# Band masks of a windowed attention: from identity products on TensorE to additions on VectorE

## The chip, the cores and the metric

The kernel runs on one core of one Trainium2 chip. The metric is the device time of one execution in microseconds; lower is better. A core has TensorE (PE, with its weight loads as PEld), VectorE (DVE), ScalarE (ACT), GpSimd (POOL) and SyncE (SP, which issues most DMAs). Every engine works through its own list of instructions in the order in which the build put them there, and waits on semaphores for the others.

## The reference

Two layers over 1024 latent tokens and 256 context tokens, model width 1024, all in float32. Layer 0 (even) has two attentions side by side, A (global) and B (windowed), each with 8 query heads on 2 key heads of width 64. What matters here is B: blocks of 128 queries look at the 256 context keys and at a band of three key blocks, of which keys farther than 128 positions are masked, and a learned sink logit joins the softmax.

```python
def gqa_attend(q, k, v, bias=None, sink=None):
    s = jnp.einsum("bqhgd,bkhd->bhgqk", q, k) * ATTN_SCALE      # ATTN_SCALE = 1/8
    if bias is not None:
        s = s + bias
    ...                                                          # sink column, softmax
    return jnp.einsum("bhgqk,bkhd->bqhgd", p, v)

# B: one block of 128 queries, band of 3 key blocks
rel = jnp.arange(band)[None, :] - B_WINDOW - jnp.arange(Q_BLOCK)[:, None]
in_band = jnp.abs(rel) <= B_WINDOW
bias = jnp.concatenate([ctx_open, jnp.where(valid, 0.0, NEG_INF)], axis=-1)
```

Of the three key blocks the middle one lies wholly in the window; the block before it and the block behind it are each masked along a triangle. Layer 1 (odd) has a convolution branch and a neighbourhood attention D whose scores get a full bias table.

## The kernel before

**Matmuls in split precision.** A float32 operand is split into a high part in the format of the products (fp32r in the profile) and a low part (`split`, lines 325 to 334: a cast on ACT, a subtraction on POOL or DVE). Three products replace one.

**Attention, `attn_gen`.** One generator runs all attention of a layer as a list of groups; a group is four heads of one key head against one block of 128 queries (layer 0), so a score tile is 128 keys by 512 (4 heads x 128 queries). For each tile, in this order: two matmuls into a PSUM bank `st` (L529 keys by `QH`; L533 keys and four extra rows by `QL`, which brings the low part of the query and minus the row's maximum), the exponential on ACT from the bank into the SBUF tile `pf` (L541, scale 1/8), the split of `pf` into `ph` (ACT, L331) and `pl` (POOL or DVE, L334), and, three tiles later (`LOOK0`), the products with the values into bank `ov` (L480 to L482). There are two `st` banks, two `pf` buffers (tag `ost` in layer 0) and four each of `ph` and `pl`.

**Masks before.** A masked tile of layer 0 gets a third matmul into its bank between L529 and L533 (L532): the mask tile `bmt` (two 128x128 triangles, 0 or a large negative number) as weights, the identity, repeated for four heads, as the moving operand. In layer 1 the neighbourhood bias already goes another way: DVE adds it from the bank to `pf` (L538), and ACT takes the exponential in place (L539).

**What stands beside it.** The key heads are worked in the order `ORDER = (2, 3, 0, 1)`: units 2 and 3 are B, 0 and 1 are A. `weave` alternates steps of the attention with steps of a filler: the projection of the next unit (`pq`, `pg` matmuls L352 to L354; transposes `trk` L932, casts and rotary work on DVE: L906 to L922, L334 on `qs` and `KAt`). Per group, `attn_prep` and `attn_fin` find row maxima ahead of the scores: matmuls into a bank `mx` (L643, L663), DVE reductions (L645, and L664 with the mask), a chain of small DVE operations on `nmt` and `se` (L439 to L446), a transpose on PE (`trn`, L457), and DVE's write of the result into `QL` (L458), which L533 needs. The end of a group is DVE's too (L490 to L493, L693, L695).

**What sets the order.** A list scheduler in the build orders each engine's instructions by priority and by its own estimates of cost. So an edit moves neighbours as well. 14 of the tiles of each B unit are masked, 28 in all.

Of the kernel before, what the change touches and what calls it, by code (L numbers as in the profile page):

```python
# [10 lines left out]
F32 = mybir.dt.float32  # L11
F32R = mybir.dt.float32r
ALU = mybir.AluOpType
AF = mybir.ActivationFunctionType
# [4 lines left out]
P = 128  # L19
# [5 lines left out]
SCALE = 0.125  # L25
# [53 lines left out]
QORD = (2, 3, 4, 0, 5, 6, 1, 7, 8, 9)  # L79
# [10 lines left out]
def tile_kernel(ctx: ExitStack, tc: tile.TileContext, a, out):  # L90
    nc = tc.nc
    VE, SC, GP, PE, SY = nc.vector, nc.scalar, nc.gpsimd, nc.tensor, nc.sync
# [20 lines left out]
    def nm(s):  # L113
        uid[0] += 1
        return f"{s}_{uid[0]}"
# [11 lines left out]
    identr = cp.tile([P, P], F32R, tag="ident", name="ident")  # L127
# [193 lines left out]
    acts, dmas, firstq = [], [], []  # L321

    @contextmanager
    def behind():

        with tc.issue_after(acts[-1].ins):
            yield
# [84 lines left out]
    def copy_k(k):  # L412
        KA, KB = Ks[k % len(Ks)]
        with behind():
            acts.append(SC.copy(KB[0:64, :], KA[0:64, :].bitcast(F32)))
# [47 lines left out]
    def attn_gen(pool, groups, vshare, look, nexts=None):  # L463

        preps = [g.prep for g in groups]
        items = [(g, t) for g in groups for t in range(len(g.tiles))]
        pend = []
        cnt = [0]

        def flush():  # L470
            g, t, ph, pl = pend.pop(0)
            k, q0, n, _ = g.tiles[t]
            if t == 0:
                g.ov = bank("ov", nm("ov"))
                if g.load_v is not None:
                    g.load_v()
            V = g.v(k)
            last = t == len(g.tiles) - 1
            o = g.ov[:, q0 : q0 + n]
            PE.matmul(o, V[:, 64:192], ph[:, :n], start=(t == 0), stop=False)  # L480
            PE.matmul(g.ov[0:64, q0 : q0 + n], V[:, 0:64], ph[:, :n], start=False, stop=False)  # L481
            PE.matmul(o, V[:, 64:192], pl[:, :n], start=False, stop=(last and g.sink is None))  # L482
            if last:
                if g.sink is not None:
                    PE.matmul(g.ov, g.skm(), g.QL[0:76, :], start=False, stop=True)
                r1 = pool.tile([P, 8, 32], F32, tag="r1", name=nm("r1"), bufs=1)
                r8 = pool.tile([P, 8], F32, tag="r8", name=nm("r8"), bufs=2)
                rb = pool.tile([P, 256], F32, tag="rb", name=nm("rb"), bufs=1)
                for e in range(2):
                    VE.transpose(r1[e * 64 : (e + 1) * 64].rearrange("p a b -> p (a b)")  # L490
                                 .rearrange("p (a q) -> p a q", a=2), g.den(g.ov[64:128, :], e))
                VE.reciprocal(r8, r1[:, :, 0])
                VE.transpose(rb, r8[:, :, None].broadcast_to([P, 8, 32]))  # L493
                g.finish(g.ov, rb)

        if layer[0]:
            for g in groups[:3]:
                queries(g, kvs[-1])
        for p in preps[:2]:
            for n_, _ in enumerate(p):  # L500
                if n_ % 2:
                    yield
        for _ in attn_fin(groups[0]):
            pass
        if layer[0]:
            groups[0].copy()
        for gi, g in enumerate(groups):
            ids = [gi + 2] if gi + 2 < len(groups) else []
            if nexts is not None and gi in nexts:
                ids = nexts[gi]  # L510
            nx = [preps[k] for k in ids]
            if gi + 1 < len(groups):
                nx.insert(1 if ids[:1] == [gi + 1] else 0, attn_fin(groups[gi + 1]))
            g.next = chain.from_iterable(nx)
            g.step = -(-(18 * len(ids) + 4) // len(g.tiles))
        for g, t in items[:AHEAD]:
            g.ahead(t)
        for x, (g, t) in enumerate(items):
            if x + AHEAD < len(items):
                items[x + AHEAD][0].ahead(items[x + AHEAD][1])  # L520
            if t == 0:
                g.start()
                if layer[0] and g.no + 3 < len(groups):
                    queries(groups[g.no + 3], kvs[-1])
            k, q0, n, extra = g.tiles[t]
            KA, KB = g.k()
            st = bank("st", nm("st"))
            cs = slice(k * P, (k + 1) * P)
            sts.append(PE.matmul(st[:, :n], KA[:, cs], g.QH[:, q0 : q0 + n], start=True, stop=False))  # L529
            if not g.bias:  # L530
                for lhs, rhs in extra():
                    PE.matmul(st[:, :n], lhs, rhs, start=False, stop=False)  # L532
            PE.matmul(st[:, :n], KB[0:68, cs], g.QL[0:68, q0 : q0 + n], start=False, stop=True)  # L533
            ph = pool.tile([P, 512], F32R, tag="ph", name=nm("ph"), bufs=look + 1)
            pl = pool.tile([P, 512], F32R, tag="pl", name=nm("pl"), bufs=look + 1)
            pf = pool.tile([P, 512], F32, tag="pf" if layer[0] else "ost", name=nm("pf"), bufs=PFB)
            if g.bias and extra is not None:
                VE.tensor_tensor(pf[:, :n], st[:, :n], extra(), op=ALU.add)  # L538
                acts.append(SC.activation(pf[:, :n], pf[:, :n], AF.Exp))  # L539
            else:  # L540
                acts.append(SC.activation(pf[:, :n], st[:, :n], AF.Exp, scale=1.0 if g.bias else SCALE))  # L541
            cnt[0] += 1
            split(pf[:, :n], ph[:, :n], pl[:, :n], "s", "v" if cnt[0] % vshare == 0 else "g")
            pend.append((g, t, ph, pl))
            if t == len(g.tiles) // 2:
                g.gate()
            for _ in range(g.step // 2):
                next(g.next, None)
            yield
            if len(pend) > look:  # L550
                flush()
            for _ in range(g.step - g.step // 2):
                next(g.next, None)
            if t == len(g.tiles) - 1:
                for _ in g.next:
                    pass
            yield
        while pend:
            flush()
            yield  # L560
# [26 lines left out]
    h = [None] * 3  # L587
# [3 lines left out]
    a0 = a0x.enter_context(tc.tile_pool(name="a0", bufs=1, reuse_waits="tile"))  # L591
    sink = const("sink", [P, 8], SC, kvp)
# [3 lines left out]
    KAs, KBs, V0s = [None] * 4, [None] * 4, [None] * 4  # L596
# [13 lines left out]
    def load_kb(u):  # L610

        for ks in (slice(0, 512), slice(512, NTOK)):
            SY.dma_start(KBs[u][0:64, ks].bitcast(F32), KAs[u][0:64, ks].bitcast(F32))
# [7 lines left out]
    def group0(u, qb):  # L621
        isb = u >= 2
# [44 lines left out]
                    yield  # L667

        def mask(m):
            return lambda: [(identr, bmt[:, m, None, :].broadcast_to([P, 4, P]))]  # L670

        def none():
            return []

        kt = [(0, none), (1, none)]
        if qb >= 2:
            if isb:
# [11 lines left out]
        def finish(ov, rb):  # L689
# [9 lines left out]
            else:  # L699
# [2 lines left out]
                split(y, oh[c][0][:, fs, o : o + P], oh[c][1][:, fs, o : o + P], "s", "v")  # L702

        hs = (u - 2) * 4
        g = Group(load_q=load_q, start=(lambda: load_kb(u)) if qb == QORD[0] else (lambda: None), bias=False, ahead=lambda t: None, gate=gate, v=lambda k: V0s[u][:, k, :], load_v=None, maxes=maxes, nmp=1 if qb < 2 else (2 if isb else 3),
                  sink=(sink[:, hs : hs + 4], sink8[:, hs : hs + 4]) if isb else None, skm=lambda: sk, k=lambda: (KAs[u], KBs[u]),
                  tiles=[(k, 0, 512, x) for k, x in kt], den=den, finish=finish)
        g.prep = attn_prep(kvp, g)
# [7 lines left out]
    with ExitStack() as p0x:  # L716
# [94 lines left out]
        with after_mod(4):  # L811
# [3 lines left out]
            VE.tensor_copy(gain5[:, 0:4, :], gain[:, None, 0:64].broadcast_to([P, 4, 64]))  # L815
            VE.tensor_copy(gain5[:, 4, :], gain[:, 64:128])
            bmask = const("k_bm", [P, 384], SY, a0)
        bmt = a0.tile([P, 2, P], F32R, tag="bmt", name="bmt")
        sk = a0.tile([76, P], F32R, tag="sk", name="sk")
        cst = a0.tile([P, 512], F32, tag="ost", name="cst", bufs=2)  # L820
        with after_mod(4):
# [147 lines left out]
        for k in range(4):  # L969
            u = ORDER[k]  # L970
            n = NSTEP[u // 2] + (12 if k == 0 else 0)
# [140 lines left out]
    with ExitStack() as l1x:  # L1112
# [242 lines left out]
        def group1(gi, hd, hf):  # L1355
            i, e = divmod(hd, 2)
            ds = slice(e * 64, (e + 1) * 64)
            bms, bss = {}, {}
# [58 lines left out]

            tiles = [(0, 0, 512, None)]
            for t, (r0, r1) in enumerate(QROWS):
                tiles.append((2 + 5 * hf + t, r0 * 32, (r1 - r0) * 32, lambda t=t: bss[t]))  # L1420
            tiles.append((1, 0, 512, None))

            def den(dn, k):
# [2 lines left out]
            def finish(ov, rb):  # L1426
# [6 lines left out]
                if i == 3:  # L1433
                    split(y[ds], od3[hf][ds, 0], od3[hf][ds, 1], "s", "v")

            g = Group(no=gi, copy=lambda: copy_k(hd), load_q=load_q, load_b=load_b, maxes=maxes, nmp=2, bias=True, ahead=ahead, sink=None, tiles=tiles, den=den, finish=finish,
                      start=start, gate=gate,
                      k=lambda: Ks[hd % len(Ks)], load_v=None, v=lambda k: Vs[gi % 2][:, k if k < 2 else k - 5 * hf, :])
            g.prep = attn_prep(kvs[-1], g)
# [295 lines left out]
```

## Time and profile before

| | |
|---|---|
| runs (3) | 1527.92, 1532.71, 1538.26 us; median 1532.71 |
| profiled execution | span 1528.5 us from its first to its last instruction; the page gives no other time for it |
| median of the runs above that span | 4.2 us |
| mean granted TensorE clock | 0.976 |
| PE busy | 1451.0 us, 95% of the span |
| PEld / DVE / ACT / POOL busy | 1167.2 / 1031.7 / 748.1 / 788.0 us |
| masked tiles' mask matmuls (L532) | 28, first at 153.6 us, last at 486.6 us |

The span and what lies around it make up a run's time; since the three runs themselves lie 10.3 us apart, the 4.2 us are no more than their scatter. A matmul's bar in the trace is longer than the time for which it holds up the next one, because matmuls overlap: the spacing of starts is the price, not the bar. In tables of stretches each engine has its busy time and, in brackets, the number of instructions; PEclk is the share of full clock that TensorE was granted.

### The profile page before, as it was taken

What the parts mean: (1) busy time and instruction counts of PE and PEld (TensorE: products, weight loads), DVE (VectorE), ACT (ScalarE), POOL (GpSimd) and SP (SyncE); (2) the same over time, 40 slices, a digit from 0 to 9 for tenths busy, and PEclk for the clock granted to TensorE, in tenths of its full rate; (3) what the DMA queues carried; (4) which work ended last, traced back from release to release, by engine and by line L of the source; (5) the groups of instructions that cost most, each with busy time, mean ns of one, the idle gap of its engine ahead of it and who ended that gap; (6) DMA issues with size and microseconds to landing.
All of it is one profiled execution on the core that took longest, in us unless ns stands there. A gap on an engine that the chain in (4) does not pass through costs nothing.

```text
span 1528.5 us, 21545 instructions
## 1 busy us (share of the span) xinstructions
PE 1451.0 (95%) x7144; PEld 1167.2 (76%) x7144; DVE 1031.7 (67%) x2095; ACT 748.1 (49%) x1418; POOL 788.0 (52%) x628
## 2 busy tenths in 40 slices
PE   6999999998998999999999889999999999989996
PEld 2786877896896777886777568888887788868775
DVE  2643566589578856457676948899848666567766
ACT  3642433443435564447646665343334455455564
POOL 3360443555454766557645665665532434364665
PEclk9999999999999999999999999999999999989998
DMA  9564325422312246121202021210484677877642
GB/s 366 201 225 135 106 69 174 135 77 88 114 56 76 85 138 210 49 69 54 59 28 66 35 67 56 62 56 28 158 253 144 207 219 240 248 222 234 178 129 110
DMA packets 154167, 199.83 MB, mean 131 GB/s; under 512 B 14716, under 2 KB 95816, under 8 KB 154056
## 3 DMA queue, kind: packets, MB, share of 16 engines
q1 hardware_dynamic: 147392, 186.88, 38.9%
q10 hardware_dynamic: 6664, 11.57, 2.3%
q8 instruction: 56, 0.92, 0.3%
q14 instruction: 55, 0.45, 0.1%
HBM read 148.07 MB, written 49.02 MB: 129 GB/s over the span
## 4 chain that ended last, share of the span: by engine, by line
PE 79%; DVE 11%; issue 3%; DMA 3%; ACT 2%; POOL 1%; ACTq 0%; SPq 0%; DVEq 0%; POOLq 0%
PE p L352 6%; PE p L354 6%; PE p L353 6%; PE ov L480 5%; PE ov L482 4%; PE ov L481 4%; PE po L352 4%; PE st L533 4%; PE st L529 4%; PE po L353 4%; PE po L354 4%; PE pq L352 4%; PE pq L353 3%; PE pq L354 3%; PE pg L352 2%
## 5 line engine op out<-in xcount | busy, mean ns | idle before, releaser
L334 POOL TENSOR_TENSOR pl<-pf,ph 128x512 fp32r<-128x512 f32 (+4 forms) x321 | 394.0, 1239 | 384.9 <-ACT ph L331 337.3
L541 ACT ACTIVATE pf<-st 128x512 f32<-128x512 f32 x284 | 166.5, 597 | 203.6 <-PE st L533 165.2
L334 POOL TENSOR_TENSOR wl<-wr,wh 128x512 fp32r<-128x512 f32 (+2 forms) x131 | 169.3, 1302 | 136.5 <-ACT wh L331 124.0
L331 ACT CAST ph<-pf 128x512 fp32r<-128x512 f32 (+4 forms) x364 | 209.5, 588 | 27.1 <-PE ov L481 15.9
L352 PE MATMUL p<-hh,wh 128*128 128x512 f32 x448 | 176.0, 393 | 3.4 <-DVE spq L1233 1.3
L353 PE MATMUL p<-hl,wh 128*128 128x512 f32 x448 | 174.5, 390 | 0.0
L354 PE MATMUL p<-hh,wl 128*128 128x512 f32 x448 | 173.0, 391 | 0.0
L480 PE MATMUL ov<-ph,Vt 128*128 128x512 f32 (+4 forms) x364 | 141.0, 387 | 4.2 <-DVE y L693 2.0
L529 PE MATMUL st<-QH,KAt 128*128 128x512 f32 (+4 forms) x364 | 140.2, 386 | 3.9 <-ACT pf L541 3.1
L482 PE MATMUL ov<-pl,Vt 128*128 128x512 f32 (+4 forms) x364 | 141.1, 388 | 2.2 <-POOL pl L334 2.1
L481 PE MATMUL ov<-ph,Vt 128*64 128x512 f32 (+4 forms) x364 | 138.9, 381 | 0.0
L533 PE MATMUL st<-QL,KBt 68*128 68x512 f32 (+4 forms) x364 | 136.4, 386 | 0.9 <-issue 0.8
L1177 DVE SCALAR_TENSOR_TENSOR cps<-U,taps,cps 128x512 f32<-128x512 f32 x184 | 125.9, 748 | 0.7
L331 ACT CAST wh<-wr 128x512 fp32r<-128x512 f32 (+2 forms) x134 | 80.9, 613 | 84.1 <-PE po L353 15.9
L352 PEld LDWEIGHTS p<-hh,wh 128*128 128x128 f32 x448 | 84.2, 188 | 21.5 <-ACT spq L1231 1.6
L656 DVE TENSOR_REDUCE mp<-mx 128x1 f32<-128x512 f32 x128 | 85.3, 681 | 19.3 <-PE mx L655 18.3
L354 PEld LDWEIGHTS p<-hh,wl 128*128 128x128 f32 x448 | 84.1, 188 | 17.4
L353 PEld LDWEIGHTS p<-hl,wh 128*128 128x128 f32 x448 | 84.2, 188 | 17.1 <-issue 0.2
L1020 DVE SCALAR_TENSOR_TENSOR x<-po,modT,x 128x512 f32<-128x512 f32 (+1 forms) x72 | 46.9, 657 | 64.0 <-PE po L354 63.5
L352 PE MATMUL pq<-wh,hh 128*128 128x384 f32 x256 | 88.2, 344 | 1.0 <-ACT hh L331 1.0
L353 PE MATMUL pq<-wl,hh 128*128 128x384 f32 x256 | 87.3, 341 | 0.0
L354 PE MATMUL pq<-wh,hl 128*128 128x384 f32 x256 | 86.6, 342 | 0.0
(287 smaller groups left out, 3417.2 us busy)
## 6 DMA issues: line engine op xcount, KB each, us to landing
mw<-in_mod_w_dram SPq DMA_DIRECT2D x16, 1024.0 KB, 5.3
Q<-qs SPq DMA_DIRECT2D x40, 256.0 KB, 2.1
QH<-Q SPq DMA_DIRECT2D x80, 128.0 KB, 2.7
mw<-in_mod_w_dram SPq DMA_DIRECT2D x16, 512.0 KB, 6.8
wr<-in_od_d_dram SPq DMA_DIRECT2D x32, 256.0 KB, 3.1
wr<-in_ev_qkv_dram SPq DMA_DIRECT2D x16, 384.0 KB, 5.0
KAt<-KD SPq DMA_DIRECT2D x16, 384.0 KB, 6.5
wr<-in_od_wo_dram SPq DMA_DIRECT2D x22, 256.0 KB, 3.4
```

Source lines behind the costliest of these rows:

```text
L331: acts.append(SC.copy(hi, src))
L334: (GP if leng == "g" else VE).tensor_tensor(lo, src, hi.bitcast(F32), op=ALU.subtract)
L352: PE.matmul(o, lh, rh, start=first, stop=False)
L353: PE.matmul(o, lh, rl, start=False, stop=False)
L354: last.append(PE.matmul(o, ll, rh, start=False, stop=end))
L480: PE.matmul(o, V[:, 64:192], ph[:, :n], start=(t == 0), stop=False)
L481: PE.matmul(g.ov[0:64, q0 : q0 + n], V[:, 0:64], ph[:, :n], start=False, stop=False)
L482: PE.matmul(o, V[:, 64:192], pl[:, :n], start=False, stop=(last and g.sink is None))
L529: sts.append(PE.matmul(st[:, :n], KA[:, cs], g.QH[:, q0 : q0 + n], start=True, stop=False))
L533: PE.matmul(st[:, :n], KB[0:68, cs], g.QL[0:68, q0 : q0 + n], start=False, stop=True)
L541: acts.append(SC.activation(pf[:, :n], st[:, :n], AF.Exp, scale=1.0 if g.bias else SCALE))
L1177: VE.scalar_tensor_tensor(pc, uc, w, pc, op0=ALU.mult, op1=ALU.add)
```

## The change

The mask of a layer-0 tile is no longer multiplied in by TensorE. `extra()` now returns the mask as a view, and one DVE `tensor_tensor` adds it on the way from the bank `st` to `pf`; ACT takes the exponential of `pf` in place, with the scale 1/8 as before. Layer 1 takes the same line, with its bias seen as one head (`nh=1`). Unmasked tiles are as they were: ACT reads the bank. `bmt` is kept in plain float32.

```diff
             sts.append(PE.matmul(st[:, :n], KA[:, cs], g.QH[:, q0 : q0 + n], start=True, stop=False))
-            if not g.bias:
-                for lhs, rhs in extra():
-                    PE.matmul(st[:, :n], lhs, rhs, start=False, stop=False)
             PE.matmul(st[:, :n], KB[0:68, cs], g.QL[0:68, q0 : q0 + n], start=False, stop=True)
...
-            if g.bias and extra is not None:
-                VE.tensor_tensor(pf[:, :n], st[:, :n], extra(), op=ALU.add)
-                acts.append(SC.activation(pf[:, :n], pf[:, :n], AF.Exp))
+            if extra is not None:
+                VE.tensor_tensor(pf[:, :n].rearrange("p (h q) -> p h q", h=g.nh), st[:, :n].rearrange("p (h q) -> p h q", h=g.nh),
+                                 extra(), op=ALU.add)
+                acts.append(SC.activation(pf[:, :n], pf[:, :n], AF.Exp, scale=1.0 if g.bias else SCALE))
             else:
                 acts.append(SC.activation(pf[:, :n], st[:, :n], AF.Exp, scale=1.0 if g.bias else SCALE))
...
         def mask(m):
-            return lambda: [(identr, bmt[:, m, None, :].broadcast_to([P, 4, P]))]
-
-        def none():
-            return []
-
+            return lambda: bmt[:, m, None, :].broadcast_to([P, 4, P])
+
+        none = None
...
-        bmt = a0.tile([P, 2, P], F32R, tag="bmt", name="bmt")
+        bmt = a0.tile([P, 2, P], F32, tag="bmt", name="bmt")
...
-                tiles.append((2 + 5 * hf + t, r0 * 32, (r1 - r0) * 32, lambda t=t: bss[t]))
+                tiles.append((2 + 5 * hf + t, r0 * 32, (r1 - r0) * 32, lambda t=t: bss[t][:, None, :]))
```

Two places show what stands where. The lines of the changed kernel are numbered four lower behind the edit (L530 there is L533 before; L535 is the new addition, L641, L643, L662 are L643, L645, L664 before).

TensorE's list at the first masked tile, `st_1474`, in the first B unit, before:

```order
L353 MATMUL pq_1340<-wl_1176,hc_171 128x384
L529 MATMUL st_1474<-QH_1180,KAt_486 128x512
L532 MATMUL st_1474<-bmt,ident 128x512
L533 MATMUL st_1474<-QL_1181,KBt_484 128x512
L457 MATMUL trn_1370<-ident,nmt_1347 12x128
L643 MATMUL mx_1397<-KAt_486,QH_1382 128x256 x2
L480 MATMUL ov_1493<-ph_1364,Vt_487 128x512
```

and now:

```order
L353 MATMUL pq_1340<-wl_1176,hc_171 128x384
L529 MATMUL st_1474<-QH_1180,KAt_486 128x512
L530 MATMUL st_1474<-QL_1181,KBt_484 128x512
L354 MATMUL pq_1340<-wh_1175,hc_171 128x384
L457 MATMUL trn_1370<-ident,nmt_1347 12x128
L641 MATMUL mx_1397<-KAt_486,QH_1382 128x256 x2
L480 MATMUL ov_1493<-ph_1364,Vt_487 128x512
```

The mask product is gone, and a projection matmul has moved up into its place.

VectorE's list where the projection of the second B unit (`qs`, `KAt`, `rt`, `pc`) meets a group's maxima (`mx`, `m`, `nmt`, `se`), before:

```order
L664 ISA mx_2996,mp_2936<-mx_2996,k_bm 128x384
L664 ISA mp_2936 128x1
L920 TENSOR_TENSOR rt_891_3996<-pc_3842,k_cs 128x320 x2
L664 ISA mx_2999,mp_2936<-mx_2999,k_bm 128x384
L664 ISA mp_2936 128x1
L922 TENSOR_TENSOR pc_3842<-pc_3842,k_cs 128x2x320
L664 ISA mx_3055,mp_2936<-mx_3055,k_bm 128x384
L664 ISA mp_2936 128x1
L334 TENSOR_TENSOR qs_4131<-trk_4127,qs_4131 128x256
L439 TENSOR_REDUCE m_667_3059<-mp_2936 128x4
L441 TENSOR_TENSOR nmt_3058<-m_667_3059,sink_161 128x4
```

and now:

```order
L535 TENSOR_TENSOR pf_3239<-st_3234,bmt 128x512
L662 ISA mx_2999,mp_2936<-mx_2999,k_bm 128x384
L662 ISA mp_2936 128x1
L916 TENSOR_TENSOR rt_891_3996<-pc_3842,k_cs 128x320 x2
L662 ISA mx_3055,mp_2936<-mx_3055,k_bm 128x384
L662 ISA mp_2936 128x1
L334 TENSOR_TENSOR qs_4131<-trk_4127,qs_4131 128x256
L918 TENSOR_TENSOR pc_3842<-pc_3842,k_cs 128x2x320
L439 TENSOR_REDUCE m_667_3059<-mp_2936 128x4
L334 TENSOR_TENSOR KAt_486<-trk_4127,KAt_486 64x128
L535 TENSOR_TENSOR pf_3332<-st_3327,bmt 128x512
L441 TENSOR_TENSOR nmt_3058<-m_667_3059,sink_161 128x4
```

Two additions now stand in this run, one of them between the maximum `m` and the chain on `nmt`, and the rotary work on `rt` and `pc` has moved back by a reduction or two.

More of the change, by code (lines that the diff above doesn't have):

```diff
@@ L704, in group0 @@
         hs = (u - 2) * 4
-        g = Group(load_q=load_q, start=(lambda: load_kb(u)) if qb == QORD[0] else (lambda: None), bias=False, ahead=lambda t: None, gate=gate, v=lambda k: V0s[u][:, k, :], load_v=None, maxes=maxes, nmp=1 if qb < 2 else (2 if isb else 3),
+        g = Group(load_q=load_q, start=(lambda: load_kb(u)) if qb == QORD[0] else (lambda: None), bias=False, nh=4, ahead=lambda t: None, gate=gate, v=lambda k: V0s[u][:, k, :], load_v=None, maxes=maxes, nmp=1 if qb < 2 else (2 if isb else 3),
                   sink=(sink[:, hs : hs + 4], sink8[:, hs : hs + 4]) if isb else None, skm=lambda: sk, k=lambda: (KAs[u], KBs[u]),
@@ L1434, in finish @@
                     split(y[ds], od3[hf][ds, 0], od3[hf][ds, 1], "s", "v")
-            g = Group(no=gi, copy=lambda: copy_k(hd), load_q=load_q, load_b=load_b, maxes=maxes, nmp=2, bias=True, ahead=ahead, sink=None, tiles=tiles, den=den, finish=finish,
+            g = Group(no=gi, copy=lambda: copy_k(hd), load_q=load_q, load_b=load_b, maxes=maxes, nmp=2, bias=True, nh=1, ahead=ahead, sink=None, tiles=tiles, den=den, finish=finish,
                       start=start, gate=gate,
```

## The prediction

> **What bounds the kernel now.** I began with the page: who is busy, and what the chain that ended last is made of.
>
> ```profile
> PE 1451.0 (95%) x7144; PEld 1167.2 (76%) x7144; DVE 1031.7 (67%) x2095; ACT 748.1 (49%) x1418; POOL 788.0 (52%) x628
> PE 79%; DVE 11%; issue 3%; DMA 3%; ACT 2%; POOL 1%; ACTq 0%; SPq 0%; DVEq 0%; POOLq 0%
> ```
>
> TensorE is the bound on the whole, and VectorE is next: 11% of the chain runs over it. The averages don't say what is so where the change sits. So next the line of the mask products, which gives the place, and the forms of the operations there, and the table of stretches for that place and for its worst spots.
>
> ```profile
> L532 PE MATMUL st<-bmt,ident x28: 389/395/403, 153.6 to 486.6; 128*128 128x512 f32 x28
> ```
>
> ```profile
> core 0: us, PE busy (x) PEld busy (x) DVE busy (x) ACT busy (x) POOL busy (x), PEclk, DMA share, GB/s
> 150.00:490.00 340.00, 330.40 (x1702) 277.99 (x1700) 232.48 (x546) 143.42 (x304) 164.37 (x123) 0.98 0.31 99
> 240.00:245.00 5.00, 3.91 (x19) 2.99 (x18) 4.92 (x15) 3.39 (x9) 2.52 (x2) 1.00 0.67 256
> 350.00:355.00 5.00, 2.82 (x14) 1.52 (x13) 4.57 (x11) 1.70 (x6) 2.76 (x2) 1.00 0.40 132
> 370.00:375.00 5.00, 3.38 (x14) 1.79 (x12) 4.77 (x12) 2.08 (x7) 3.94 (x3) 0.88 0.32 107
> 375.00:380.00 5.00, 4.71 (x13) 3.76 (x13) 4.36 (x12) 2.61 (x5) 1.70 (x2) 0.50 0.33 108
> 380.00:385.00 5.00, 5.00 (x22) 4.03 (x21) 2.83 (x7) 0.81 (x3) 0.82 (x1) 0.93 0.25 83
> 460.00:475.00 15.00, 12.46 (x57) 9.71 (x56) 13.23 (x30) 5.87 (x11) 7.12 (x5) 0.93 0.12 35
> 485.00:490.00 5.00, 4.19 (x18) 2.57 (x17) 4.81 (x11) 4.06 (x9) 2.73 (x3) 1.00 0.39 106
> ```
>
> The B units take 340 us. TensorE is idle for 9.6 of them (340 - 330.4), VectorE is 68% busy. So most of the stage is bound by TensorE, and a matmul less is a matmul's time less. But the idle time is not spread: it lies where VectorE has no gap. In the five rows from 240 to 245, 350 to 355, 370 to 375, 460 to 475 and 485 to 490 VectorE is busy 4.92, 4.57, 4.77, 13.23 (of 15) and 4.81 us, and TensorE waits for it. The clock row from 375 to 380 says that such a hole is paid twice: there the granted clock is 0.50.
>
> The timeline of TensorE and of VectorE at the third of these shows how the waiting goes:
>
> ```profile
> 370.45 0.41 DVE L334 TENSOR_TENSOR qs<-trk,qs 128x256 fp32r<-128x256 f32 x1
> 371.26 1.47 DVE L443 SCALAR_TENSOR_TENSOR se<-nmt,sink 128x4 f32<-128x4 f32 x1
> 372.75 0.28 DVE L334 TENSOR_TENSOR KAt<-trk,KAt 64x128 fp32r<-64x128 f32 x1
> 373.19 0.52 PE L932 MATMUL trk<-ident,pc 128*128 128x128 f32 x3 [1.43 <-DVE KAt L334]
> 375.37 0.80 PE L643 MATMUL mx<-KAt,QH 128*128 128x256 f32 x2 [0.29 <-DVE QL L458]
> ```
>
> VectorE works off the projection's `qs` and `KAt` and the group's `se` in one row, and TensorE, whose list is fixed, stands 1.43 us before a transpose whose bank `KAt` has not left yet.
>
> **The change, part by part.** *Removed from TensorE:* 28 matmuls. The bar of 395 ns is not the price; the distance of starts is.
>
> ```profile
> 300.30 0.40 PE L529 MATMUL st<-QH,KAt 128*128 128x512 f32 x1
> 300.53 0.40 PE L532 MATMUL st<-bmt,ident 128*128 128x512 f32 x1
> 300.77 0.40 PE L533 MATMUL st<-QL,KBt 68*128 68x512 f32 x1
> ```
>
> From 300.30 to 300.77 two starts pass, 0.235 us each; the weight load lies under the matmul before. 28 x 0.235 = **6.6 us** less on TensorE, 0.4% of the span.
>
> *Added to VectorE:* 28 additions of 128x512 from the bank. Layer 1 does the same operation, so its row has the price, and the rows of ACT's two kinds of exponential:
>
> ```profile
> L538 DVE TENSOR_TENSOR pf<-st,bs 128x512 f32<-128x512 f32 x16 | 10.8, 673 | 0.3 <-PE ov L481 0.2
> L539 ACT ACTIVATE pf<-pf 128x512 f32<-128x512 f32 x16 | 10.1, 631 | 18.9 <-DVE pf L538 16.8 <-DVE rb L493 2.0
> L541 ACT ACTIVATE pf<-st 128x512 f32<-128x512 f32 x82 | 46.7, 596 | 79.8 <-PE st L533 76.3 <-POOL pl L334 2.7 <-POOL Vt L914 0.6
> ```
>
> 28 x 0.673 = 18.8 us, which brings VectorE from 232.5 to 251.3 of 340 us, 74%. The mask is a view repeated over four heads instead of a dense bias; no row of before has that form on two inputs of 128x512, and I take the price as the same. ACT's exponential costs 631 - 596 = 35 ns more, 1.0 us in all, on an engine that is busy for 143 of 340 us and idle 79.8 us before these very exponentials: nothing; without that cover 1.0 us.
>
> What of the 18.8 us is on the path? In the order of the changed kernel I looked for the additions that stand in the five runs without a gap. There are nine: one at the first, one at the second, two at the third (both shown with the change), two in the fourth, three in the last and just ahead of it. The other 19 lie where VectorE has idle time, and cost nothing there. The nine can cost from 0 to 9 x 0.673 = 6.1 us. For the upper end speaks the third place, where additions stand ahead of `KAt` and `se`, for which TensorE waits already. For the lower end speaks that two of the nine stand behind the last write of `nmt` and ahead of `QL`, where VectorE waits for a transpose anyway:
>
> ```profile
> 472.50 0.68 DVE L458 TENSOR_TENSOR QL<-trn,k_bd 12x512 fp32r<-12x512 f32 x1 [0.37 <-PE trn L457]
> 482.52 0.68 DVE L458 TENSOR_TENSOR QL<-trn,k_bd 12x512 fp32r<-12x512 f32 x1 [0.49 <-PE trn L457]
> ```
>
> I take half, **+3.0 us**.
>
> *A new wait:* the addition waits for its scores, and for `pf` to be left by the subtraction two tiles before; formerly ACT stood in that wait. Queued behind it on VectorE now are the reductions of `mx`, `qs`, `KAt` and the `nmt` chain, for which TensorE's `trk`, `trn`, L643 and L663 wait. In layer 1 the same wait shows so:
>
> ```profile
>   POOL pl L334: 8.8, 8
>   PE st L533: 5.2, 6
>   ACT pf L539: 61.4, 43
>   PEld st L529: 1.6, 3
>   PE st L529: 0.6, 2
> ```
>
> The first two rows are VectorE's idle time ahead of 80 additions, 14.0 us; the last three are who waited for them: ACT much, TensorE and its weight loads 2.2 us. Scaled to 28 additions that is 4.9 us of idle VectorE and 28/80 x 2.2 = **0.8 us** of TensorE. I take the 0.8. Its upper bound is in the rival below. The lower is nothing: the bank `st` may even come free sooner, as an addition needs no turn in ACT's list.
>
> *Moved:* the list scheduler shifts neighbours by a few rows; no DMA is added or dropped, and where SP issues `QH` or `gt` a few places away, the rows of DMA share (0.31 in the stage) leave room. I cost this at nothing. The cast of `bmt` becomes a copy, once: nothing.
>
> **The sum**: -6.6 + 3.0 + 0.8 = **-2.8 us** against the span of 1528.5, so 1525.7. The runs' median stands 4.2 us above that span, and I carry the difference over: 1532.7 - 2.8 = **1529.9 us**. Own bounds: if no addition is on the path, -6.6 + 0 + 0 = -6.6; if all nine are, and the nine removed matmuls there bring nothing since TensorE waits anyway (+2.1), -6.6 + 6.1 + 0.8 + 2.1 = +2.4.
>
> **The rivals.**
>
> *VectorE becomes the bound in the B units (slower).* The place is the run of the third row above and all like it; the price is 0.673 us for each addition on the path, and it decides from 6.6 / 0.673 = 10 additions on. For it: VectorE's list is fixed too, and an addition that waits for a late score keeps everything behind it. ACT now idles 76.3 us before 82 exponentials for scores, 0.93 each, and 28 of these waits move to VectorE: 26 us on an engine that has 107.5 idle. Against it: those 107.5 us are more than 18.8 + 26, and layer 1's row shows TensorE little troubled. With 18 on the path +12.1 - 6.6 = +5.5, 1538; with all 28, +12.2, 1545.
>
> *Holes grow until the clock falls (slower).* From the rows: the hole before 375 costs 5 x 0.50 + 5 x 0.12 + 5 x 0.07 = 3.5 us of clock around it. The holes at 350 and 460, now at 1.00 and 0.93, each get additions. If both fall in the same way, -2.8 + 7.0 = +4.2, 1537. [...]
>
> *The clock is regained (faster).* The same hole may close: the neighbours shift, and 3.5 us, with 15 x 0.07 = 1.1 from the row of 460, come back on top of the 6.6: -11.2, 1521.5. For it: it takes only a shift of a microsecond at 372. Against it: two additions have come just there.
>
> *Nothing comes of it.* The matmuls are gone from TensorE's list, so the change does what it says. But what follows may wait for something else, the freed 6.6 us turning into waits for `pl` or for VectorE: 0, 1532.7.
>
> **How the numbers follow.** Forecast 0.50; VectorE the bound 0.18; clock falls 0.10; clock regained 0.10; nothing 0.12. The range reaches from the regained clock to VectorE's full bound, and on the low side by 2.5 us farther, half of the 4.8 us by which the fastest run lies under the median: **1519 to 1545**. A measurement of this kernel can tell about 1% from no change, 15.3 us, since three runs of it lie 10.3 us apart. No case alone gives 15.3 us on the fast side; regained clock and scatter together might: faster 0.10. On the slow side all additions on the path with a fallen clock give 12.2 + 3.5 = 15.7 us: slower 0.14. Within 1%: **0.76**.
>
> **What would show it.** Right: no mask matmul; TensorE's busy time in the B units shorter by about 6 us; 28 additions near 673 ns; VectorE at 74% there; idle TensorE in the stage between 9 and 14 us, at the same five places; the rest of layer 0 and layer 1 as long as before. Wrong: additions at a price far from 673 ns; idle TensorE over 16 us, with the additions as the releaser or just ahead of it on VectorE (the first rival); the clock at 0.50 in more than one stretch (the second) or in none (the third); the stages after 490 us changed by more than 3 us, which none of my cases has, and which would mean that the shifted neighbours matter more than the operations.

## The result, and the profile after

The changed kernel takes **1544.85 us** (median of 6 runs, 1542.32 to 1546.19), the kernel before 1533.23 us (6 runs, the three given above among them). The ratio is 1.0076, 95% interval [1.0055, 1.0096]: 11.6 us slower, where 2.8 us faster was forecast. The time itself lies inside the stated range, at the end (1545) that the first rival gave to all 28 additions on the path; it is not there by the forecast's sum. The profiled execution took 1542.32 us; its span is 1540.5 us, so 1.8 us lie around it.

One sentence of the description above has two operands the wrong way round: in the mask product the identity `identr` is the stationary weights and the mask `bmt`, repeated for four heads, the moving operand. The spacing of starts, from which its price was taken, is as measured there.

First the page of the changed kernel, busy time by engine and the chain that ended last:

```profile
PE 1452.6 (94%) x7116; PEld 1162.8 (75%) x7116; DVE 1047.2 (68%) x2123; ACT 748.4 (49%) x1418; POOL 789.2 (51%) x628
PE 78%; DVE 10%; issue 3%; DMA 3%; POOL 2%; ACT 2%; SPq 0%; ACTq 0%; DVEq 0%; POOLq 0%
```

28 matmuls fewer, 28 operations on VectorE more, and TensorE's busy time is not shorter: a bar of 128x512 that takes 0.40 us at 469.38, at full clock, takes 0.63 us at 475.22, where the clock is 0.50. The groups of the changed kernel between 150 and 500 us show the new operations; columns are busy us, mean ns, and idle time ahead with what ended it:

```profile
L535 DVE TENSOR_TENSOR pf<-st,bmt 128x512 f32<-128x512 f32 x28 | 19.1, 683 | 4.3 <-PE st L530 4.0
L537 ACT ACTIVATE pf<-pf 128x512 f32<-128x512 f32 x28 | 17.7, 631 | 38.8 <-DVE pf L535 38.8
L539 ACT ACTIVATE pf<-st 128x512 f32<-128x512 f32 x56 | 31.8, 596 | 55.4 <-PE st L530 47.7 <-DVE pl L334 3.9 <-POOL pl L334 3.8
```

The prices are those forecast: 683 ns for 673, and 631 ns on ScalarE. VectorE idles 4.3 us ahead of the additions, where 4.9 were scaled from layer 1. New is the second row's end: ScalarE now stands 38.8 us behind VectorE. The stretches of the prediction, in the changed kernel:

```profile
150.00:490.00 340.00, 327.05 (x1671) 270.23 (x1672) 247.08 (x573) 143.12 (x303) 160.30 (x120) 0.98 0.31 98
240.00:245.00 5.00, 5.00 (x24) 4.10 (x23) 4.67 (x13) 1.65 (x5) 2.55 (x2) 1.00 1.05 406
350.00:355.00 5.00, 4.38 (x14) 1.38 (x14) 3.28 (x7) 0.91 (x3) 4.11 (x4) 0.66 0.17 37
370.00:375.00 5.00, 2.94 (x10) 1.29 (x10) 4.90 (x11) 2.25 (x6) 4.08 (x3) 1.00 0.32 105
375.00:380.00 5.00, 3.77 (x22) 3.00 (x23) 4.52 (x11) 3.46 (x9) 2.07 (x3) 1.00 0.22 81
460.00:475.00 15.00, 10.11 (x36) 5.78 (x35) 14.39 (x30) 5.79 (x11) 5.43 (x4) 0.86 0.12 35
```

Over the whole stage this looks like the forecast: idle TensorE 340 - 327.05 = 12.95 us (9 to 14 forecast), VectorE 247.08 of 340, 73%. The five holes did not stay, though: the one at 240 closed, the fall of the clock at 375 went (0.50 to 1.00), one at 350 came (0.66), and the stretch from 460 to 475 has 10.11 us of TensorE for 12.46.

To find where the time goes, I took the same matmul in both traces and subtracted its two times of start. The changed kernel is 2.6 us *ahead* at 440 us of the kernel before, 4.5 us behind at 480 to 500, 8.2 us behind at 540, and 11.4 us behind from 900 to 1100 us. So **10.8 us are lost between 440 and 540 us**, at the end of the second B unit and just behind it. The same 100 us in the two kernels, before first:

```profile
440.00:540.00 100.00, 93.14 (x470) 76.64 (x469) 83.93 (x174) 47.90 (x101) 58.29 (x45) 0.98 0.25 80
```

```profile
440.00:540.00 100.00, 87.85 (x416) 69.27 (x415) 85.18 (x173) 44.25 (x94) 54.76 (x43) 0.93 0.23 73
```

TensorE idles 5.3 us more, and its clock is 0.05 lower over 100 us: 100 x 0.05 = 5.0 us more at most, an estimate from these two rows that counts the waits as if they were work. So about half of the loss is waiting, and up to half the clock that fell with the waiting. What TensorE waits for there, before and after (us in total, times, longest):

```profile
PE mx L655 <- DVE mp L656: 1.7, 3, 1.0
PE ov L482 <- POOL pl L334: 1.2, 1, 1.2
PE mx L663 <- DVE mp L645: 0.9, 1, 0.9
...
PE trn L457 <- DVE nmt L446: 0.5, 1, 0.5
PE st L529 <- ACT pf L541: 0.4, 1, 0.4
```

```profile
PE mx L653 <- DVE mp L654: 3.2, 2, 2.7
PE trn L457 <- DVE nmt L446: 2.2, 2, 1.9
PE st L529 <- DVE m L439: 1.7, 1, 1.7
PE ov L482 <- DVE pl L334: 1.0, 1, 1.0
PE ov L480 <- ACT ph L331: 0.9, 2, 0.7
PE st L529 <- ACT pf L539: 0.9, 2, 0.5
```

All rows of this view add up to 6.7 us before and 11.7 us after. Three waits grew: for a maximum `mp` (2.7 us at once), for the chain on `nmt`, and a score matmul that waits for VectorE, which it never did before in layer 0. The last one is read in the timeline of the changed kernel, VectorE and TensorE:

```profile
480.91 0.69 DVE L535 TENSOR_TENSOR pf<-st,bmt 128x512 f32<-128x512 f32 x1
481.62 0.12 DVE L439 TENSOR_REDUCE m<-mp 128x4 f32<-128x8 f32 x1
481.74 0.47 PE L529 MATMUL st<-QH,KAt 128*128 128x512 f32 x1 [1.73 <-DVE m L439]
```

A score matmul does not read `m`; it needs a bank. The addition that empties a bank ended at 481.60, and TensorE started 0.14 us later. In five such places of three traces (this one, two in e5, two in e10) the start comes 0.14 to 0.15 us behind an addition's end, while the distance to the end of `m` varies from 0.00 to 0.09. So the row's releaser is best read as the addition.

The longest wait of the stretch, 2.7 us until 524.00 for `mp`, has no addition in it. A small operation of the projection, `nr`, stands ahead of the maximum on VectorE; first the changed kernel, with what GpSimd does beside it, then the kernel before, where it comes behind the first of two maxima:

```profile
521.30 1.19 DVE L252 SCALAR_TENSOR_TENSOR nr<-nt,nr 128x10 f32<-128x10 f32 x1
519.95 2.50 POOL L334 TENSOR_TENSOR pl<-pf,ph 128x512 fp32r<-128x512 f32 x2
```

```profile
517.27 0.37 DVE L252 SCALAR_TENSOR_TENSOR nr<-nt,nr 128x10 f32<-128x10 f32 x1
```

Ten columns take 1.19 us here, and the operation ends 0.04 us after GpSimd's; where no GpSimd operation is running beside it, `nr` takes 0.13 to 0.17 us in both traces. So a part of what counts as busy on VectorE in these holes is operations that take longer than elsewhere while one of GpSimd's is running (more of this in the last section).

### The profile page after: what moved, and what is told of

Its sections match the earlier page's. It is cut to its first block, busy times and chain, and to the rows that moved or that the text cites. A ratio compares the mean times of both kernels' runs of the same rounds, so it can differ in the third digit from the quotient of the medians.

```text
span 1540.5 us, 21532 instructions
## 1 busy us (share of the span) xinstructions
PE 1452.6 (94%) x7116; PEld 1162.8 (75%) x7116; DVE 1047.2 (68%) x2123; ACT 748.4 (49%) x1418; POOL 789.2 (51%) x628
## 4 chain that ended last, share of the span: by engine, by line
PE 78%; DVE 10%; issue 3%; DMA 3%; POOL 2%; ACT 2%; SPq 0%; ACTq 0%; DVEq 0%; POOLq 0%
PE p L352 6%; PE p L354 6%; PE p L353 6%; PE ov L480 5%; PE ov L482 4%; PE ov L481 4%; PE st L530 4%; PE st L529 4%; PE po L352 4%; PE po L354 4%; PE po L353 4%; PE pq L354 3%; PE pq L353 3%; PE pq L352 3%; PE pm L185 3%
## 5 line engine op out<-in xcount | busy, mean ns | idle before, releaser
L539 ACT ACTIVATE pf<-st 128x512 f32<-128x512 f32 x256 | 150.2, 596 | 184.3 <-PE st L530 128.4
L530 PE MATMUL st<-QL,KBt 68*128 68x512 f32 (+4 forms) x364 | 137.1, 387 | 0.9 <-issue 0.8
L537 ACT ACTIVATE pf<-pf 128x512 f32<-128x512 f32 (+4 forms) x108 | 55.8, 519 | 101.9 <-DVE pf L535 97.6
L529 PEld LDWEIGHTS st<-QH,KAt 128*128 128x128 f32 x364 | 69.8, 192 | 28.0 <-ACT pf L539 8.6
L482 PEld LDWEIGHTS ov<-pl,Vt 128*128 128x128 f32 x364 | 70.4, 193 | 25.5 <-POOL pl L334 3.9
```

## The experiments

Two causes were at hand: the additions on VectorE, and the new order of everything else, which the build's scheduler made. The first four runs vary the work and leave the order to the scheduler; the next ones hold the order fixed.

**Half of the change.** Masks of one B unit by VectorE, of the other by products (`e2` is the reverse of `e1`).

```diff
+            if isinstance(extra, tuple):
+                PE.matmul(st[:, :n], extra[0], extra[1], start=False, stop=False)
+                extra = None
...
+            if u == 2:
+                return lambda: bmt[:, m, None, :].broadcast_to([P, 4, P])
+            return (identr, bmr[:, m, None, :].broadcast_to([P, 4, P]))
```

> The masks of the first B unit (unit 2) are added by VectorE, those of the second (unit 3) stay identity products on TensorE. Theory 1 (one place: the run without a gap on VectorE at the end of unit 3, 450 to 540 us, costs the time; the first unit gains): 14 matmuls less and no stall there, 2 to 4 us faster than before, about 1530. Theory 2 (every addition costs alike, 11.6 us over 28): 5.8 us slower, about 1539. Theory 3 (the shifted order costs, not the additions): anything, and the two halves do not add up to 11.6.

> The other half: unit 3 by VectorE, unit 2 by identity products. Theory 1: all of the loss, 10 to 15 us slower than before, with TensorE idle and at half clock between 450 and 540 us. Theory 2: 5.8 us slower. Theory 3: anything.

Measured: 1533.89 us, ratio 1.0005 [0.9972, 1.0037], and 1531.98 us, 0.9998 [0.9972, 1.0025]. Neither half costs what the whole does: together 0.5 us, some 6 us either way, against 11.6. That can't come from a price per addition alone, nor from the additions of the second unit at its end (theory 1); theory 3, the order, is left.

**The last groups by products.** All by VectorE, but for blocks 7, 8 and 9 of unit 3, whose five additions stand between 468 and 494 us.

```diff
+            if not (u == 3 and qb >= 7):
+                return lambda: bmt[:, m, None, :].broadcast_to([P, 4, P])
+            return (identr, bmr[:, m, None, :].broadcast_to([P, 4, P]))
```

> VectorE adds all masks but the five of the last three query blocks of unit 3 (blocks 7, 8, 9), which stay identity products. Theory 1: those five stand in the run without a gap; without them the loss is gone, 0 to 5 us faster than before, 1528 to 1533. Theory 2: 23/28 of 11.6, 9.5 us slower, about 1543. Theory 3: no forecast.

Measured: 1539.22 us, 1.0064 [1.0042, 1.0086]. Most of the loss stays without the additions that stand at its place. In its trace less of it lies there, though: by the same subtraction about 5 us are lost between 440 and 540 us, and about 6 between 860 and 900.

**No mask by anyone.** Neither product nor addition; the masked tiles' exponential has scale 0, so these tiles' part of the result is left out.

```diff
+            if extra == 0.0:
+                acts.append(SC.activation(pf[:, :n], st[:, :n], AF.Exp, scale=0.0))
```

> No mask at all: neither product nor addition; ACT reads the bank and takes the exponential with scale 0 in the masked tiles, so that the time is that of an unmasked tile and the result of these tiles is left out. Theories 1 and 2: the 28 matmuls are gone and VectorE has nothing more, 6.6 us faster or a little more, about 1526. Theory 3: the order is shifted here too, so the loss may come without any addition: slower than 1528.

Measured: 1540.05 us, 1.0057 [1.0038, 1.0076]. **A kernel with strictly less work is 8.7 us slower.** So an addition isn't needed for a loss. In its trace it comes in two places, about 7 us between 440 and 540 us and about 7 more between 860 and 900; the second was not looked into. What is left is the order, or a thinner row of matmuls. The waits of TensorE between 440 and 540 us in this kernel begin with:

```profile
PE trn L457 <- DVE nmt L446: 4.6, 1, 4.6
PE mx L655 <- DVE mp L656: 1.4, 3, 0.9
```

**The work and the order apart.** Each engine's instructions are chained in a table's order, by order of issue alone; the masks (products or additions) stay free. The traces show that it holds: but for the masks, the lists of TensorE, VectorE, GpSimd and SyncE in e5 and e7 are those of the kernel before, row for row, and those in e6 are the changed kernel's. The edit is one call, `pin(nc, tc)` behind the traced kernel, and the table:

```diff
+        pin(nc, tc)
+        for a, b in zip(order, order[1:]):
+            tc.add_manual_dep(own[b], own[a].name, NoSync, ...)
```

The change's work in before's order:

> The change's work in the order of before: on each engine the instructions are chained, by issue order alone, in the sequence that the build gave the kernel before; only the 28 additions find their own places on VectorE. Order theory (the shifted order costs, not the work): no loss is left, 3 to 7 us faster than before. Work theory (the additions on VectorE cost): 8 to 12 us slower, like the change. Thin-TensorE theory (28 matmuls less let the clock fall): slower too, with a lower granted clock than before.

Before's work in the changed kernel's order (ScalarE free):

> The reverse: the work of before, identity products and all, with TensorE, VectorE, GpSimd and SyncE chained in the order of the changed kernel (ScalarE left free; the 28 products find their own places). Order theory: slower than before by 8 us or more, with the hole between 450 and 540 us. Work theory and thin-TensorE theory: as before, within 3 us.

No mask, in before's order:

> No mask by any engine (ScalarE's exponential with scale 0 in the masked tiles, whose result is left out), chained in the order of before. Order theory: the 28 products alone are gone, 5 to 8 us faster than before, against 8 us slower in its own order. Work theory: faster as well, it cannot explain the loss in its own order. Thin-TensorE theory: slower, as without the chaining.

Before's work in the order of the kernel without a mask:

> The work of before, chained on all engines in the order that the build gave the kernel without masks. Order theory: slower than before, by the 8 us of that kernel and up to 6.6 more for the products that are back: 1539 to 1546. Other theories: as before, within 3 us.

Measured, as ratios to the kernel before:

| work | before's order | the changed kernel's order | order of the kernel without a mask |
|---|---|---|---|
| products | 1 | 1.0095 [1.0066, 1.0125] (e6) | 1.0077 [1.0049, 1.0105] (e8) |
| no mask | 0.9973 [0.9949, 0.9997] (e7) | | 1.0057 [1.0038, 1.0076] (e4) |
| additions | 1.0050 [1.0030, 1.0070] (e5) | 1.0076 [1.0055, 1.0096] (the change) | |

Read by rows, the order alone costs 0.95% with products (14.5 us) and 0.84% without a mask (12.9 us); with additions it costs 0.26%, 4.0 us, which is not clear of the noise. Without a mask and in the old order the kernel is 4.1 us *faster* than before, so fewer matmuls do no harm, and the thin-TensorE theory falls. Read by columns: in the changed kernel's order additions for products come out 0.19% lower, 2.9 us, but the two intervals leave that some 5 us either way, so it may be nothing; in before's order they lose 7.7 us, and against no mask at all they cost 0.77%, 11.8 us.

So neither theory holds alone. The order theory foresaw e6, e8 and, within its interval, e7, and fails in e5, where it had 3 to 7 us faster; the work theory fails in e6 and e8. **Either cause is enough by itself, and they do not add up**: 14.5 us for the order and 7.7 for the additions would make 22, and the change loses 11.6. One limit: e5 holds ScalarE's list fixed too, and ScalarE stands 63.0 us behind additions there (150 to 500 us) against 38.8 in the changed kernel; what of the 7.7 us is due to that was not taken apart.

**Which additions.** In before's order: the 19 additions that the prediction put at nothing on VectorE, the nine in its gapless runs as products, and the reverse.

```diff
+            if not (u == 3 and qb in (2, 3, 7, 8, 9) or u == 2 and qb == 6 and m == 0):
+                return lambda: bmt[:, m, None, :].broadcast_to([P, 4, P])
+            return (identr, bmr[:, m, None, :].broadcast_to([P, 4, P]))
```

> In the order of before: the 19 masks that the prediction placed where VectorE has idle time are added by VectorE, the nine in its runs without a gap stay identity products. Place theory (an addition costs where VectorE has no gap, and nothing elsewhere): 19 x 0.235 = 4.5 us faster than before, 3 to 6. Even theory (the change in the old order is about 8 us slower than before and about 12 slower than no mask at all, spread over all 28): 19/28 of 8, 5 us slower.

> The counterpart in the order of before: the nine on VectorE, the 19 as identity products. Place theory: the whole loss of the additions, 8 to 12 us slower than before. Even theory: 9/28 of 8, 2 to 3 us slower.

Measured: 1.0023 [1.0005, 1.0041] for the 19, 1.0032 [1.0013, 1.0052] for the nine. Each kernel also drops its products, at 0.235 us each or less, so the nine cost 4.9 us and up to 2.1 more, some 0.5 to 0.8 us apiece, about their own 0.68; the 19 cost 3.5 us and up to 4.5 more, 0.2 to 0.4 us apiece. The place theory fails in both (3 to 6 us faster for the 19, 8 to 12 slower for the nine); the even theory comes nearer. That an addition in a gapless run costs more than another is likely, but the intervals, some 2 to 3 us either way on each kernel, do not settle it. The nine show how in the timeline, VectorE, ScalarE and TensorE:

```profile
470.36 0.68 DVE L538 TENSOR_TENSOR pf<-st,bmt 128x512 f32<-128x512 f32 x1
471.07 0.63 ACT L540 ACTIVATE pf<-pf 128x512 f32<-128x512 f32 x1 [3.92 <-DVE pf L538]
471.19 0.47 PE L529 MATMUL st<-QH,KAt 128*128 128x512 f32 x1 [1.93 <-DVE m L439]
```

```profile
467.01 0.40 PE L529 MATMUL st<-QH,KAt 128*128 128x512 f32 x1
467.24 0.40 PE L533 MATMUL st<-QL,KBt 68*128 68x512 f32 x1
```

The last scores ahead of the addition were out by 467.64, and no other score matmul starts until 471.19. VectorE comes to the addition at 470.36, behind rotary work, a subtraction and four maxima. Only then do a bank come free and the exponential start, 3.2 us behind the addition's own scores (the pair ahead of these two, out by 467.17). In the kernel before, the masked scores at this place are out by 465.98, and ScalarE starts on them 0.8 us later:

```profile
466.76 0.60 ACT L541 ACTIVATE pf<-st 128x512 f32<-128x512 f32 x1 [1.03 <-POOL pl L334]
```

**One place.** Before's work and order, but what started between 425 and 500 us stands in the sequence of the kernel without a mask; and that kernel with its own stretch from 420 to 500 us in before's sequence.

> The work and the order of before, but for one stretch: what started between 425 and 500 us stands, on every engine, in the sequence that it has in the kernel without masks, in which the rotary work of the last projection block is ahead of the chain of a group's maxima on VectorE. Window theory (the shifted order costs in this one place): 7 to 10 us slower than before. Spread theory (many places cost a little): 1 to 3 us slower.

> The kernel without masks (exponential with scale 0 in the masked tiles, result left out) in its own order, but for that stretch (420 to 500 us in its trace), which stands in the sequence of before. Window theory: its 8 us of loss fall to 2 or less, or turn into a gain. Spread theory: 5 to 8 us slower than before stay.

Measured: 1.0050 [1.0031, 1.0069], 7.7 us of the 11.8 that the whole order costs; and 1.0034 [1.0018, 1.0050] for 1.0057, 3.5 us less, of the 12.9 that the order costs without a mask. The first fits the window theory, the second the spread theory (5.2 us slower than before stay), and its 3.5 us are not clear of the noise. By these two a stretch of 75 to 80 us holds a quarter to two thirds of the order's cost. Then the same with the changed kernel: its stretch from 420 to 545 us back in before's sequence; its sequence of that stretch in the kernel before; and back up to 500 us only.

> The changed kernel in its own order, but what started between 420 and 545 us in its trace stands in before's sequence on every engine (the additions stay free). If the loss of the change is this stretch's order: about 8 us off the 11.6, so a ratio near 1.002 to before, and no loss of arrival between 450 and 540 us. If the additions themselves are the loss there: no gain, 1.007. If the order costs the same everywhere, a quarter of 340 us off: 1.005.

> The work of before in before's order, but what started between 420 and 545 us stands in the changed kernel's sequence on TensorE, VectorE, GpSimd and SyncE (ScalarE free); no additions. If this stretch's order is the loss: 6 to 9 us, ratio 1.004 to 1.006, with the loss between 450 and 540 us. If it needs the additions: 1.000.

> As e13, but only the stretch from 420 to 500 us is taken back to before's sequence. If the cause sits before 490 us and the rest follows from it: like e13, near 1.002. If the stretch from 500 to 545 us has an order cost of its own: between e13 and the change, 1.004 to 1.006.

Measured: 1.0070 [1.0056, 1.0085], 1.0043 [1.0026, 1.0059] and 1.0082 [1.0066, 1.0099]. The first expectation of e13 (1.002) fails, the second holds: with the additions there, the old sequence brings nothing. Both numbers expected of e15 fail: it is no faster than the change either. e14 shows the other side: without an addition, the new sequence of this stretch alone costs 6.6 us. The waits of TensorE between 440 and 540 us in e14, and then in e13, show two different ways into the same hole:

```profile
PE mx L655 <- DVE mp L656: 3.2, 2, 2.7
PE trn L457 <- DVE nmt L446: 1.7, 1, 1.7
PE ov L480 <- DVE y L693: 1.4, 2, 1.1
PE ov L482 <- DVE pl L334: 1.0, 1, 1.0
```

```profile
PE st L529 <- DVE m L439: 3.6, 2, 2.3
PE mx L653 <- DVE mp L654: 2.2, 4, 1.0
PE mx L661 <- DVE mp L643: 1.4, 2, 1.2
```

By the new sequence TensorE waits for maxima, `nmt` and `y`, since other VectorE work stands ahead of them; by the additions it waits for banks, and for maxima too. The totals are alike, 9.4 and 9.7 us for 6.7 before. VectorE is 84% busy in either, and in the changed kernel, which has both, TensorE waits little longer (11.7 us).

**The bank given back by ScalarE.** If the bank were all, a copy by ScalarE, which has time there, ahead of the addition would mend it.

```diff
+                if not g.bias:
+                    SC.copy(pf[:, :n], st[:, :n])
+                    src = pf
```

> All engines in before's order. ScalarE copies the masked scores from the bank to pf, VectorE adds the mask in place in pf, ScalarE takes the exponential in place: 28 additions as in the change, 28 copies more on ScalarE (some 0.6 us each, which idles before these). If the late return of the bank is what the additions cost: TensorE's waits for an addition before a score go, most of the 8 us between 440 and 540 us go, ratio 0.998 to 1.001. If VectorE's time is what counts: 1.005 as with the addition from the bank. If the longer chain of a tile counts (copy, addition, exponential): over 1.007.

> The same work in the order that the build gives it. If the bank is the one cause: 0.998 to 1.002, as e16. If order has its own cost, as without a mask: 1.004 to 1.008.

Measured: 1557.10 us, 1.0162 [1.0137, 1.0187] in before's order, and 1547.31 us, 1.0101 [1.0074, 1.0127] in its own. e16 fits its third case, the longer chain of a tile; e17 is slower than either of its cases. The first row of TensorE's waits between 440 and 540 us in e16, and its additions between 150 and 500 us:

```profile
PE ov L480 <- ACT ph L331: 4.7, 3, 2.2
```

```profile
L539 DVE TENSOR_TENSOR pf<-pf,bmt 128x512 f32<-128x512 f32 x26 | 21.5, 827 | 3.6 <-ACT pf L537 3.6
```

No score waits for an addition any more, as expected; the wait has gone one step on. `ph` comes from the exponential, which still stands behind the addition and now behind a copy as well, and TensorE waits for that. The bank alone is not the cause: whatever hands the tile over, its chain runs through a VectorE that comes late. Of these 24 us, 28 x (0.827 - 0.683) = 4.0 us at most are the dearer addition, and in the build's own order 9.8 us less are lost; how much of the rest is the copy and how much ScalarE's fixed list was not taken apart.

**Not measured.** An addition could also stand late since its `pf` is not free yet; no run has a third `pf` buffer. The changed kernel's row of additions leaves little for it: of the 4.3 us that VectorE idles ahead of them, 4.0 are for scores.

## Why the prediction was wrong, step by step

Two steps failed, and each alone turns the forecast's -2.8 us into a loss.

- **"Moved: ... I cost this at nothing" is the first step that failed.** The order, with before's own work, costs 14.5 us (e6; interval 10 to 19), more than the whole change. The rows of DMA share, on which the nothing was based, say nothing of it: what was shifted is VectorE's work on `mp`, `nmt` and `y` against rotary work. The prediction did name the sign of it, "the stages after 490 us changed by more than 3 us": from 480 to 500 until 540 us the lag grows by another 3.7 us.
- **The removed products, -6.6 us.** In before's order they bring -4.1 us (e7, 0.5 to 7.8): right within its interval.
- **What of the additions is on the path, +3.0 us, is the second.** In before's order, where nothing else has moved, the sum of -2.8 us is measured as +7.7 (e5, 4.6 to 10.7). The additions cost 11.8 us there (e5 against e7, some 5 us either way) for the +3.0 and the +0.8 together. "The other 19 lie where VectorE has idle time, and cost nothing there" does not hold: these 19 make the kernel 3.5 us slower (e9) where 4.5 faster follow from it. An addition's wait for its turn (3.2 us in the rows of e10), more than its 0.67 us, is what holds up banks and exponentials. Its own price was right (683 ns for 673).
- **The new wait, +0.8 us with "the bank `st` may even come free sooner":** the direction was wrong. The bank comes free later: scores wait 2.2 us for additions in the changed kernel (1.73 of them at once) and 3.8 us in e13, between 440 and 540 us, because an addition needs a turn in a list without a gap, where ScalarE had time.
- **The first rival** had the right engine and a right price, but put it on the additions alone; e4 and e14 lose at the same place without any. That its 1545 for all 28 meets the measured time is in part luck: the change's loss is made of two causes that overlap. **The third**, the clock regained, happened in part: the fall at 375 us is gone and a shorter one at 350 has come (2.6 us ahead at 440, the products that are gone included), and the next hole took it back.
- **The clock, the second rival**, is up to half of the loss at the place, 5.0 us. It is read here as no cause of its own, since it follows the holes. Two stretches, in the changed kernel and in e14, and the longest wait of TensorE in the changed kernel between 455 and 500 us:

```profile
470.00:475.00 5.00, 2.63 (x8) 1.68 (x9) 4.53 (x10) 2.26 (x5) 2.49 (x2) 0.59 0.17 52
```

```profile
470.00:480.00 10.00, 7.32 (x20) 4.95 (x21) 6.78 (x14) 2.54 (x5) 4.94 (x4) 0.61 0.18 54
```

```profile
473.27 0.38 PE L457 MATMUL trn<-ident,nmt 128*12 128x128 f32 x1 [1.89 <-DVE nmt L446]
```

In the changed kernel no wait there is longer than 1.89 us, and the clock is 0.59 from 470 to 475. The wait of 1.89 us, from 471.38 on, comes too late to be the reason: the clock falls at 470.87, and in the 15 us until then no wait is longer than 0.97 us:

```profile
467.50:470.90 3.40, 2.08 (x7) 1.09 (x7) 3.29 (x11) 2.32 (x4) 0.40 (x1) 1.00 0.18 47
470.90:474.30 3.40, 1.51 (x6) 1.00 (x5) 3.06 (x5) 0.70 (x3) 2.09 (x2) 0.50 0.21 69
```

What lies ahead of the fall is three waits close together, of 0.59, 0.97 and 0.70 us, and TensorE is busy for 2.08 of the last 3.40 us.

What stays open: why the two halves of the change, each with an order of its own, cost nothing; how the two causes share the 11.6 us; and where the order's cost lies outside the stretches that were exchanged (a third of it by e11, three quarters by e12, with steps of 6 to 7 us between 860 and 900 us in e3 and e4). A version faster than the kernel before was not among the complete ones.

## What to carry to other kernels

Where a scheduler orders the lists, an edit is a new order first and an operation's price second: freeze the old order and time the new work in it, and time the old work in the new order, before a loss or a gain is put down to the operation. An engine that is 68% busy on average can be busy for 17.0 of 20 us (455 to 475 us in the kernel before), and there a mere change of sequence costs as much as work does (6.6 us in e14); look in those stretches at who hands buffers back, and be slow to move that duty from an engine that has time to one that has none.

## What the runs showed of the hardware

- The runs of the kernel before follow the granted clock. 31 of them on one chip (beside e1 to e4) had spans from 1523.0 to 1545.0 us at mean clocks from 0.983 down to 0.963, with a correlation of -0.92, some 0.95 us for 0.001 of clock. On the four other chips (11 to 28 runs, beside e5 to e17) the correlation is -0.65 to -0.78. Ten microseconds between two single runs of this kernel say little without the clock beside them.
- In the traces of the kernel before and of the changed one, every stretch at clock 0.50, but for the last of each trace, is 3.41 us long (15 of them), 6.83 (11) or 10.24 (one). Cut the two traces between 140 and 600 us into such steps of 3.41 us, starting where the clock changes, and take the 258 at full clock: of the 15 in which TensorE was busy for less than 70%, seven were followed by half clock, of the 243 others none. In two of these seven falls (at 470.87 and 494.76 us in the changed kernel) no pause within the step reached 1 us.
- The same addition took 683 ns from the score bank and 827 ns on average (26 in its view: shortest 648, median 684, longest 1694) with both inputs in SBUF (e16). One of these, with what GpSimd does beside it:

```profile
482.83 1.05 DVE L539 TENSOR_TENSOR pf<-pf,bmt 128x512 f32<-128x512 f32 x1
```

```profile
481.39 1.94 POOL L924 TENSOR_TENSOR pc<-pc,rt 128x640 f32<-128x640 f32 x1 [2.56 <-DVE pc L922]
```

GpSimd's operation ends at 483.33, and the addition at 483.88, 0.55 us later. In the changed kernel six additions began with 0.5 us or more of a GpSimd operation to run, and none took over 0.69; there one input comes from the bank. By these figures, 683 ns for 827, reading one input from the bank was the better choice in the change.
- Some of the smallest operations end with GpSimd's too. `se` (L443, 128x4, two inputs in SBUF) takes 0.15 to 0.16 us in the kernel before when no GpSimd operation is running. In six of the seven places in the kernel before where one is, it takes 0.45 to 1.47 us and ends 0.02 us after GpSimd's; the 1.47 us at 371.26, in the hole that the prediction shows, is one of them. So VectorE's busy share holds time by which its operations are longer there than elsewhere: by an estimate from the same operations' lengths in the same trace where no GpSimd operation is running, some 14 us of its 83.93 between 440 and 540 us in the kernel before and 15 of 85.18 in the changed one. What moving GpSimd's work would bring was not tried.
